# Heads of 64: the value's high and low part as one weight of 128 columns, two passes for three, and the halves added on VectorE

## The chip, the cores and the metric

The kernel runs on one core of one Trainium2 chip. The metric is the device time of one launch in microseconds. The profile is one execution of the kernel before, read instruction by instruction: PE is TensorE's matmul, PEld its weight load, DVE is VectorE, ACT is ScalarE, POOL is GpSimd, SP issues most transfers.

## What is computed

The reference is a whole small model over 512 rows of width 1024, in fp32. The first half has two layers: an attention, a cross attention on a memory of 256 rows, and a gated feed-forward network each. The second half is one layer with a "forgetting" attention beside a pooling mixer, and a convolved feed-forward network. The change touches the two attentions whose values are 64 wide and whose scores are dense and causal:

```
# first layer (MLA): 16 heads, queries and keys 96 wide, values 64 wide
logits = jnp.einsum('bqhd,bkhd->bhqk', q_blk, k).astype(jnp.float32) * scale
logits = jnp.where(causal[None, None], logits, -jnp.inf)
p = jax.nn.softmax(logits, axis=-1).astype(v.dtype)
return jnp.einsum('bhqk,bkhd->bqhd', p, v)
...
# second half (fox): 8 heads, queries, keys and values 64 wide
s = s + Fi[..., None] - Fk[:, :, None, :]
s = jnp.where(qpos[:, None] >= kpos[None, :], s, -jnp.inf)
p = jax.nn.softmax(s, axis=-1)
return jnp.einsum('bhqk,bkhd->bqhd', p, v32)
```

## The kernel before

Every fp32 operand of a matmul is held as a pair of fp32r tiles, a high part and a low part. `split` (L157 to L161) makes a pair: ScalarE casts the source to the high part (L160), and VectorE subtracts the high part from the source for the low part (L161). `mm3` (L151 to L155) multiplies two pairs in three passes, high by high (L153), high by low (L154), low by high (L155).

`attention` (L666 and on) serves both stretches. Per head it has four steps. `s1` computes the scores of four row blocks (tile `s`, 12 matmuls), takes mask and row minimum in one operation on VectorE (L685, tile `P`, or `p` for the block of 256), and the exponential on ScalarE (L687). `norm` takes the reciprocal of the row sums on VectorE (L693) and multiplies on GpSimd (L696). `s2` transposes the probabilities on TensorE (L704, ten transposes, tiles `t`) and splits them into three pairs `pt`. `s3` multiplies by the values: one PSUM tile `o`, whose partitions 0 to 63 are the head's 64 columns, collects four key blocks by `mm3`, with 512, 384, 256 and 128 rows of queries; the weight is the 64 columns of the value (tile `v`), and the moving operand is `pt`. So one head has 12 matmuls for `o`, and then `split` writes half a pair of `ot`, which is the input of the projection after the attention.

The loop over heads is a software pipeline. Iteration h issues `s3(h - lag)`, `s2(h - 2)`, `norm(h - 1)`, `s1(h)`, and then other work that fills TensorE: for MLA the projections of queries and keys for two heads more at every even h below 14 (36 matmuls, tile `qk`), and by the tables `FILL_V` and `FILL_A` parts of the values and of the cross attention's keys and values (tiles `v`, `k`); for fox the pooling mixer (tile `pl`). The lag is 3 for MLA and 4 for fox. PSUM has 8 buffers that all tiles share. A scheduler at build time orders the instructions of each engine from this program; at run time each engine works through its own list, and waits at each instruction for what it needs.

MLA's attention lies at about 85 to 230 us of the span, fox at about 1700 to 1778 us. During MLA the low parts of the weights (`wl`, L122) are made on GpSimd.

Of the kernel before, what the change touches and what calls it, by code (L numbers as in the profile page):

```python
# [9 lines left out]
F = mybir.dt.float32  # L10
R = mybir.dt.float32r
# [3 lines left out]
OP = mybir.AluOpType  # L15
# [4 lines left out]
NT = 4  # L20
# [44 lines left out]
class K:  # L65
# [416 lines left out]
    def mla(self):  # L482
        nc, a = self.nc, self.a
        xd = a["x"][0].rearrange("(t p) d -> p t d", p=128)
        xs = []
        for t in range(NT):
            x = self.pg(F, "x0")
# [98 lines left out]
        V = {}  # L586
        st = {}

        def vproj(h, js=range(NT)):
            if js[0] == 0:  # L590
                st["v"] = self.use()
            u = st["v"]
            for j in js:
                p = self.ps("v")
                g, c = j // 2, slice((j % 2) * 128, (j % 2) * 128 + 128)
                for k in range(2):
                    self.mm3(p, [ckv[g][0][:, k, c], ckv[g][1][:, k, c]], [u[0][:, k], u[1][:, k]], k == 0, k == 1)
                V[h, j] = self.pair("v")
                self.split(V[h, j][:, 0], V[h, j][:, 1], p)

        kr = self.pair("kr")
        self.rope(krf, kr)
# [10 lines left out]
        for i in range(2):  # L613
            nc.scalar.dma_start(KF[i][0][64:96].bitcast(F), kr[64:96].bitcast(F))
            nc.scalar.dma_start(KF[i][1][32:64].bitcast(F), kr[32:64].bitcast(F))
        OT = []
        vproj(0)

        def proj(p):
# [35 lines left out]
        def fill(h):  # L655
            if h in FILL_V:
                vproj(1, FILL_V[h])
            self.fill(FILL_A.get(h, 0))
        self.attention(16, rowsel, lambda h: [V[h // 8, j][:, :, (h % 8) * 64:(h % 8) * 64 + 64] for j in range(NT)],
                       OT, scale, ahead,  # L660
                       None, fill)
        self.ahead, self.dma_ahead = AHEAD, DMA_AHEAD
        self.lo_eng = nc.vector
        return OT

    def attention(self, nh, rows, vals, OT, scale, ahead, before3=None, fill=None, lag=3):  # L666

        nc = self.nc
        A = {}

        def s1(h):
            q, k = rows(h)
            p0, p1, p2 = self.ps("s"), self.ps("s"), self.ps("s")
            sv = [p0[:, 0:128], p1[:, 0:256], p0[:, 128:512], p2[:, 0:512]]
            pa = self.pg(F, "P")
            pb = self.cp.tile([128, 256], F, tag="p1", bufs=3, name=self.nm("p1"))
            pv = [pa[:, 896:1024], pb, pa[:, 512:896], pa[:, 0:512]]
            sm = self.small(16, "st")
            for b in (3, 2, 0, 1):
                nk = (b + 1) * 128  # L680
                c = slice(b * 128, b * 128 + 128)
                self.mm3(sv[b], [q[:, 0, c], q[:, 1, c]], [k[:, 0, 0:nk], k[:, 1, 0:nk]], True, True)
            for b in (3, 2, 0, 1):
                nk = (b + 1) * 128
                nc.vector.tensor_tensor_reduce(out=pv[b], in0=sv[b], in1=self.mask[:, 512 - nk:512], scale=-scale,  # L685
                                               scalar=3.0e38, op0=OP.add, op1=OP.min, accum_out=sm[:, b:b + 1])
                nc.scalar.activation(pv[b], pv[b], AF.Exp, bias=sm[:, b:b + 1], scale=-1.0,  # L687
                                     accum_out=sm[:, 4 + b:5 + b])
            A[h] = dict(pv=pv, sm=sm)

        def norm(h):
            sm, pv = A[h]["sm"], A[h]["pv"]
            nc.vector.reciprocal(sm[:, 8:12], sm[:, 4:8])  # L693
            for b in (3, 2, 0, 1):
                nk = (b + 1) * 128
                nc.gpsimd.tensor_tensor(pv[b], pv[b], sm[:, 8 + b:9 + b].to_broadcast([128, nk]), op=OP.mult)  # L696

        def s2(h):
            pv = A[h]["pv"]
            t0, t1, t2 = self.ps("t"), self.ps("t"), self.ps("t")  # L700
            tv = [t0[:, 0:512], t1[:, 0:384], t2[:, 0:256], t1[:, 384:512]]
            for j in (3, 1, 2, 0):
                for b in range(j, 4):
                    nc.tensor.transpose(tv[j][:, (b - j) * 128:(b - j + 1) * 128], pv[b][:, j * 128:(j + 1) * 128],  # L704
                                        self.ident)
            g1, g0 = self.pair("pt"), self.pair("pt")
            g2 = self.cp.tile([128, 512], R, tag="pt2", bufs=2, name=self.nm("pt2")).rearrange("p (h n) -> p h n", h=2)
            self.split(g1[:, 0], g1[:, 1], t1)
            self.split(g2[:, 0], g2[:, 1], t2[:, 0:256])
            self.split(g0[:, 0], g0[:, 1], t0)  # L710
            A[h]["pt"] = [g0[:, :, 0:512], g1[:, :, 0:384], g2, g1[:, :, 384:512]]

        def s3(h):
            v, pt = vals(h), A[h]["pt"]
            o = self.ps("o")
            for j in range(NT):
                self.mm3(o[0:64, 128 * j:512], [v[j][:, 0], v[j][:, 1]], [pt[j][:, 0], pt[j][:, 1]], j == 0, j == 3)
            if h % 2 == 0:
                OT.append(self.pair("ot"))
            r = slice(64 * (h % 2), 64 * (h % 2) + 64)  # L720
            self.split(OT[h // 2][r, 0], OT[h // 2][r, 1], o[0:64])
            del A[h]

        for h in range(nh + lag):
            if 0 <= h - lag < nh:
                if before3 is not None:
                    before3(h - lag)
                s3(h - lag)
            if 0 <= h - 2 < nh:
                s2(h - 2)  # L730
            if 0 <= h - 1 < nh:
                norm(h - 1)
            if h < nh:
                s1(h)
                ahead(h)
            if fill is not None:
                fill(h)
# [107 lines left out]
    def fill(self, n=1):  # L845

        if self.kvs is None:
            self.kvs = self.xa_kv_steps()
        for _ in range(n):
            next(self.kvs, None)  # L850
# [536 lines left out]
    def second(self, xT, xn, xs):  # L1387
        nc, a = self.nc, self.a
        v = nc.vector
# [32 lines left out]
        p = fz[0]  # L1422
# [23 lines left out]
        vp = [self.ps("v") for _ in range(NT)]  # L1446
        for kk in range(4):
            u = self.use()
            for j in range(NT):
                c = slice(j * 128, j * 128 + 128)  # L1450
                for k in range(2):
                    x = xT[2 * kk + k]
                    self.mm3(vp[j], [x[:, 0, c], x[:, 1, c]], [u[0][:, k], u[1][:, k]], kk + k == 0, kk == 3 and k == 1)
        V = []
        for j in range(NT):
            V.append(self.pair("v"))
            self.split(V[j][:, 0], V[j][:, 1], vp[j])
        QF, KF = [], []

        def rings():  # L1460
# [24 lines left out]
        def pool_mm(g, mp, pw):  # L1485
            p = self.ps("pl")
            self.mm3(p, [pw[0][:, g], pw[1][:, g]], [mp[:, 0], mp[:, 1]], True, True)
            o = mixed[4 + g] = self.pair("mx")
            sc = self.col2[:, 64 + g:65 + g]
            nc.scalar.activation(o[:, 0], p, AF.Copy, scale=sc)  # L1490
            v.scalar_tensor_tensor(o[:, 1], p, sc, o[:, 0].bitcast(F), op0=OP.mult, op1=OP.subtract)

        OT = []
# [11 lines left out]
        def pools(h):  # L1505
            if h == min(FILL_P):
                pw.append(self.use())
            for g in FILL_P.get(h, ()):
                pool_mm(g, mps[g], pw[0])
        self.attention(8, rows, lambda h: [V[j][:, :, h * 64:h * 64 + 64] for j in range(NT)], OT, 1.0, before,  # L1510
                       fill=pools, lag=4)
        self.ahead, self.dma_ahead = AHEAD, DMA_AHEAD
        for k in range(4):
# [158 lines left out]
```

## Time and profile before

| what | value |
|---|---|
| time, median of 3 runs | 2203.94 us (2202.64 to 2204.45) |
| the profiled execution | 2198.25 us, span 2196.2 us |
| mean granted clock of TensorE | 0.987 of full |
| PE busy | 2144.8 us, 98% of the span |
| VectorE, ScalarE, GpSimd busy | 1353.9, 898.8, 294.2 us |

The span runs from the first to the last instruction on the chip; the profiled execution has 2.05 us around it. Busy time of PE is the union of its matmuls, which overlap in the pipeline: the cost of one matmul among others is the time from its start to the start of the next, and not the duration in its row.

### The profile page before, as it was taken

To read this page: it belongs to the slowest core of one execution; us is meant where nothing else is said; L and a number is where in the kernel's file an instruction comes from. 1 tells how busy PE (TensorE), PEld (TensorE's weight loads), DVE (VectorE), ACT (ScalarE), POOL (GpSimd) and SP (SyncE) were. 2 spreads that over 40 slices of the span, in tenths; PEclk is the share of its full clock that TensorE was granted. 3 is DMA by queue.
4 is the path that set the end of the run, shared out by engine and by line. 5 is a ranking of instruction groups with operands and counts; after the bars stand their busy time and mean duration, and the time that the engine had idled before them with its cause. 6 is when DMAs were issued, how large, how long until landed. Compare 5 with 4: busy or idle time off the path is not lost.

```text
span 2196.2 us, 30394 instructions
## 1 busy us (share of the span) xinstructions
PE 2144.8 (98%) x11668; PEld 1798.5 (82%) x11668; DVE 1353.9 (62%) x2819; ACT 898.8 (41%) x1636; POOL 294.2 (13%) x290
## 2 busy tenths in 40 slices
PE   8899999999999999899999999999999999999998
PEld 7789898988888887776689898888888879888886
DVE  5776566835237267898875855436377676765634
ACT  3677444312224043456634332224324555443521
POOL 0355100000000012365500000000003210000002
PEclk9999999999999998999999999999999999999999
DMA  5223613355334132230251355534320144433311
GB/s 192 63 66 93 208 58 115 104 156 162 88 109 141 54 97 64 77 113 29 82 163 59 106 173 173 153 115 163 106 58 20 45 125 145 141 91 100 128 58 39
DMA packets 253393, 232.28 MB, mean 106 GB/s; under 512 B 14656, under 2 KB 219840, under 8 KB 253248
## 3 DMA queue, kind: packets, MB, share of 16 engines
q1 hardware_dynamic: 246240, 213.93, 31.9%
q10 hardware_dynamic: 7008, 16.41, 2.2%
q8 instruction: 92, 1.51, 0.3%
q14 instruction: 53, 0.43, 0.1%
HBM read 220.80 MB, written 6.82 MB: 104 GB/s over the span
## 4 chain that ended last, share of the span: by engine, by line
PE 85%; DVE 6%; issue 1%; ACT 1%; POOL 1%; DMA 0%; ACTq 0%; SPq 0%; DVEq 0%; POOLq 0%
PE fm L154 14%; PE fm L153 14%; PE fm L155 14%; PE acc L154 9%; PE acc L155 9%; PE acc L153 9%; PE v L153 1%; PE v L154 1%; PE o L153 1%; PE v L155 1%; PE o L154 1%; PE o L155 1%; PE s L1241 1%; PE tp L232 1%; PE s L155 1%
## 5 line engine op out<-in xcount | busy, mean ns | idle before, releaser
L154 PE MATMUL fm<-xT,wh 128*128 128x512 f32 (+3 forms) x1640 | 589.6, 361 | 0.4
L155 PE MATMUL fm<-xT,wl 128*128 128x512 f32 (+3 forms) x1640 | 588.9, 359 | 0.0
L153 PE MATMUL fm<-xT,wh 128*128 128x512 f32 (+3 forms) x1640 | 588.5, 361 | 0.1
L122 DVE TENSOR_TENSOR wl<-raw,wh 128x1024 fp32r<-128x1024 f32 (+1 forms) x299 | 357.0, 1218 | 93.4 <-ACT wh L121 63.9
L121 ACT CAST wh<-raw 128x1024 fp32r<-128x1024 f32 (+2 forms) x339 | 339.0, 1039 | 65.6 <-PE acc L154 18.9
L154 PEld LDWEIGHTS fm<-xT,wh 128*128 128x128 f32 (+2 forms) x1640 | 307.9, 188 | 48.5 <-DVE xT L250 1.6
L155 PEld LDWEIGHTS fm<-xT,wl 128*128 128x128 f32 (+2 forms) x1640 | 307.9, 188 | 46.9
L153 PEld LDWEIGHTS fm<-xT,wh 128*128 128x128 f32 (+2 forms) x1640 | 307.1, 188 | 47.9 <-DVE xT L249 0.6
L122 POOL TENSOR_TENSOR wl<-raw,wh 128x1024 fp32r<-128x1024 f32 (+1 forms) x40 | 93.7, 2348 | 1228.5 <-ACT wh L121 614.5
L153 PE MATMUL acc<-wh,hs 128*128 128x512 f32 x528 | 205.6, 389 | 0.0
L154 PE MATMUL acc<-wl,hs 128*128 128x512 f32 x528 | 205.4, 389 | 0.0
L155 PE MATMUL acc<-wh,hs 128*128 128x512 f32 x528 | 204.9, 389 | 0.0
L967 DVE TENSOR_TENSOR hT<-sil,fm 128x512 f32<-128x512 f32 x44 | 30.3, 688 | 228.9 <-PE fm L155 215.5
L966 ACT ACTIVATE sil<-fm 128x512 f32<-128x512 f32 x44 | 26.3, 598 | 300.6 <-PE fm L155 283.5
L950 DVE SCALAR_TENSOR_TENSOR cv<-fm,cw,cv 128x511 f32<-128x511 f32 x88 | 65.7, 748 | 81.7 <-ACT cv L948 80.5
L153 PEld LDWEIGHTS acc<-wh,hs 128*128 128x128 f32 x528 | 99.1, 188 | 20.7
L155 PEld LDWEIGHTS acc<-wh,hs 128*128 128x128 f32 x528 | 99.1, 188 | 20.5
L154 PEld LDWEIGHTS acc<-wl,hs 128*128 128x128 f32 x528 | 99.1, 188 | 20.4
L153 PE MATMUL acc<-wh,ot 128*128 128x512 f32 x288 | 112.5, 391 | 0.0
L155 PE MATMUL acc<-wh,ot 128*128 128x512 f32 x288 | 112.1, 389 | 0.0
L154 PE MATMUL acc<-wl,ot 128*128 128x512 f32 x288 | 112.1, 389 | 0.0
L217 ACT ACTIVATE x<-x,mv 128x1024 f32<-128x1024 f32 x20 | 24.9, 1243 | 147.4 <-DVE mv L216 147.4
(366 smaller groups left out, 3660.0 us busy)
## 6 DMA issues: line engine op xcount, KB each, us to landing
raw<-in_ffn_w_in_dram SPq DMA_DIRECT2D x88, 512.0 KB, 4.0
mw<-in_mod_w_dram SPq DMA_DIRECT2D x48, 512.0 KB, 4.8
raw<-in_ffn_w_down_dram SPq DMA_DIRECT2D x44, 512.0 KB, 3.3
raw<-in_ffn_up_dram SPq DMA_DIRECT2D x44, 512.0 KB, 4.0
raw<-in_xa_w_kv_dram SPq DMA_DIRECT2D x32, 512.0 KB, 3.9
raw<-in_ffn_down_dram SPq DMA_DIRECT2D x22, 512.0 KB, 3.3
raw<-in_xa_w_q_dram SPq DMA_DIRECT2D x16, 512.0 KB, 5.3
raw<-in_xa_w_o_dram SPq DMA_DIRECT2D x16, 512.0 KB, 3.2
```

The lines of the kernel that those rows point to most:

```text
L121: self.nc.scalar.copy(hi[:, :n], raw[:, :n])
L122: self.lo_eng.tensor_tensor(lo[:, :n], raw[:, :n], hi[:, :n].bitcast(F), op=OP.subtract)
L153: mm(out, l[0], r[0], start=first, stop=False, **kw)
L154: mm(out, l[0], r[1], start=False, stop=False, **kw)
L155: mm(out, l[1], r[0], start=False, stop=last, **kw)
L217: ops.append(lambda: nc.scalar.activation(x, x, AF.Identity, bias=mv[:, 3:4], scale=mv[:, 2:3]))
L232: nc.tensor.transpose(st["ps"][:, g, tl * 128:(tl + 1) * 128], xs[2 * grp + tl][:, (f + g) * 128:(f + g + 1) * 128], self.ident)
L950: nc.vector.scalar_tensor_tensor(y[:, sh:], p[:, :S - sh], w[:, 2 - sh, c:c + 1], y[:, sh:], op0=OP.mult, op1=OP.add)
L966: nc.scalar.activation(s, g, AF.Silu)
L967: nc.vector.tensor_tensor(hT[j // 2][:, j % 2], s, u, op=OP.mult)
L1241: mm(p[32 * gq:32 * gq + 32, 0:nk], D3[:, i, hf], mv[:, gq, 0:nk], start=False, stop=i == 2, skip_group_check=True)
```

## The change

The values are stored head by head, 64 columns of the high part and then the 64 of the low part of the same head, so that one weight of 128 columns holds both. The product of a key block is then two matmuls in place of three, one with the high and one with the low part of the probabilities as the moving operand. Partitions 0 to 63 of `o` collect what the high part of the value gives, partitions 64 to 127 what the low part gives (the product of both low parts, which `mm3` left out, is now in it). ScalarE copies partitions 64 to 127 to an SBUF tile `oy`, VectorE adds partitions 0 to 63 to it, and the pair of `ot` is split from `oy` in SBUF and not from `o` in PSUM.

```
+    @staticmethod
+    def hp64(v):
+        return v.rearrange("p (a b c) -> p a b c", a=8, b=2)
+
+    def vsplit(self, p):
+        v = self.pg(R, "v")
+        x = self.hp64(v)
+        self.split(x[:, :, 0], x[:, :, 1], p.rearrange("p (a c) -> p a c", a=8))
+        return v
...
# where the values are made, MLA
-                V[h, j] = self.pair("v")
-                self.split(V[h, j][:, 0], V[h, j][:, 1], p)
+                V[h, j] = self.vsplit(p)
...
# where the values are made, fox
-            V.append(self.pair("v"))
-            self.split(V[j][:, 0], V[j][:, 1], vp[j])
+            V.append(self.vsplit(vp[j]))
...
# s3
             for j in range(NT):
-                self.mm3(o[0:64, 128 * j:512], [v[j][:, 0], v[j][:, 1]], [pt[j][:, 0], pt[j][:, 1]], j == 0, j == 3)
+                for i in range(2):
+                    nc.tensor.matmul(o[:, 128 * j:512], v[j], pt[j][:, i], start=j == 0 and i == 0, stop=j == 3 and i == 1)
             if h % 2 == 0:
                 OT.append(self.pair("ot"))
             r = slice(64 * (h % 2), 64 * (h % 2) + 64)
-            self.split(OT[h // 2][r, 0], OT[h // 2][r, 1], o[0:64])
+            y = self.cp.tile([128, 512], F, tag="hp", bufs=3, name=self.nm("oy"))
+            nc.scalar.copy(y[r], o[64:128])
+            nc.vector.tensor_tensor(y[r], o[0:64], y[r], op=OP.add)
+            self.split(OT[h // 2][r, 0], OT[h // 2][r, 1], y[r])
```

In the changed kernel the matmuls of `o` are at L729, the copy at L734, the add at L735; L685, L693 and L704 of the kernel before are L696, L704 and L715 there. The order of SP's transfers is the same in both. On the other engines the lists differ in the two attention stretches alone.

VectorE, MLA, where the value product of head 4 (`o_1500` before, `o_1496` after) is split while the scores of head 7 (`P_1546`, `p_1547` before, `P_1541`, `p_1542` after) are reduced. In the kernel before:

```order
L161 TENSOR_TENSOR ot_1513<-o_1500,ot_1513 64x512
L161 TENSOR_TENSOR kf_587<-qk_1454,kf_587 64x512
L161 TENSOR_TENSOR qf_583<-qk_1471,qf_583 64x512
L161 TENSOR_TENSOR pt_1529<-t_1517,pt_1529 128x512
L161 TENSOR_TENSOR pt_1531<-t_1518,pt_1531 128x256
L161 TENSOR_TENSOR pt_1530<-t_1516,pt_1530 128x512
L685 ISA P_1546,st_1548<-s_1545,cst 128x512
```

In the changed kernel:

```order
L735 TENSOR_TENSOR oy_1506<-o_1496,oy_1506 64x512
L161 TENSOR_TENSOR pt_1526<-t_1513,pt_1526 128x256
L161 TENSOR_TENSOR qf_583<-qk_1467,qf_583 64x512
L696 ISA p_1542,st_1543<-s_1539,cst 128x256
L161 TENSOR_TENSOR ot_1505<-oy_1506,ot_1505 64x512
L161 TENSOR_TENSOR pt_1524<-t_1512,pt_1524 128x512
L161 TENSOR_TENSOR pt_1525<-t_1511,pt_1525 128x512
L696 ISA P_1541,st_1543<-s_1540,cst 128x512
```

The subtraction for `ot` has become an add for `oy` and a later subtraction; the reduction of the score block of 256, which came last of its head's four, now stands ahead of both large `pt` of the head whose value product is next.

TensorE at the next head's value product (head 5: `o_1569` before, `o_1564` after), right behind the score matmuls of head 7. In the kernel before:

```order
L155 MATMUL s_1544<-kf_589,qf_585 128x256
L153 MATMUL o_1569<-pt_1530,v_751 64x512
L704 MATMUL t_1585<-cst,P_1417 128x128
L704 MATMUL t_1585<-cst,p_1418 128x128
...
L154 MATMUL o_1569<-pt_1530,v_751 64x512
L155 MATMUL o_1569<-pt_1530,v_751 64x512
```

In the changed kernel:

```order
L155 MATMUL s_1539<-kf_589,qf_585 128x256
L729 MATMUL o_1564<-pt_1525,v_751 128x512
L715 MATMUL t_1579<-cst,P_1413 128x128
L715 MATMUL t_1579<-cst,p_1414 128x128
L729 MATMUL o_1564<-pt_1525,v_751 128x512
L729 MATMUL o_1564<-pt_1524,v_761 128x384 x2
```

Both take one matmul with the high part of `pt` and then transposes of head 6 (`t_1585`, `t_1579`) until the low part is there. Before, all ten transposes stand in that gap; now two do, and the other eight come behind the value product.

## Rows read from the trace of the kernel before

**Rows 1.** The page: busy time of the engines; the chain that ended last, by engine.
```profile
PE 2144.8 (98%) x11668; PEld 1798.5 (82%) x11668; DVE 1353.9 (62%) x2819; ACT 898.8 (41%) x1636; POOL 294.2 (13%) x290
...
PE 85%; DVE 6%; issue 1%; ACT 1%; POOL 1%; DMA 0%; ACTq 0%; SPq 0%; DVEq 0%; POOLq 0%
```

**Rows 2.** Windows: stretch, its length, busy time (instructions), granted clock, DMA share, GB/s.
```profile
103.00:121.00 18.00, 18.00 (x123) 16.03 (x122) 13.94 (x36) 13.10 (x33) 9.53 (x11) 1.00 0.09 20
121.00:167.00 46.00, 43.79 (x327) 39.68 (x326) 35.99 (x99) 36.72 (x91) 28.09 (x31) 1.00 0.29 79
167.00:200.00 33.00, 32.96 (x250) 30.29 (x248) 21.63 (x55) 22.97 (x54) 16.45 (x17) 1.00 0.33 95
200.00:230.00 30.00, 29.46 (x223) 27.25 (x224) 15.02 (x35) 19.43 (x40) 20.45 (x16) 1.00 0.43 147
230.00:290.00 60.00, 60.00 (x272) 49.78 (x271) 36.91 (x69) 20.28 (x23) 0.00 (x0) 1.00 0.46 149
...
1749.00:1778.00 29.00, 27.13 (x185) 22.43 (x183) 22.70 (x55) 22.19 (x53) 8.26 (x12) 1.00 0.48 155
```

**Rows 3.** Timeline of PE, head 0's value product: start us, duration us, instruction.
```profile
102.82 0.39 PE L153 MATMUL o<-pt,v 128*64 128x512 f32 x1
...
103.50 0.34 PE L153 MATMUL o<-pt,v 128*64 128x384 f32 x1
...
104.02 0.28 PE L153 MATMUL o<-pt,v 128*64 128x256 f32 x1
...
104.36 0.22 PE L153 MATMUL o<-pt,v 128*64 128x128 f32 x1
...
104.54 0.29 PE L704 MATMUL t<-cst,P 128*128 128x128 f32 x1
```

**Rows 4.** Timeline of PE, matmuls with weights of 128 columns.
```profile
97.81 0.23 PE L153 MATMUL s<-kf,qf 96*128 96x128 f32 x1
97.87 0.28 PE L154 MATMUL s<-kf,qf 96*128 96x128 f32 x1
...
98.10 0.34 PE L153 MATMUL s<-kf,qf 96*128 96x256 f32 x1
...
98.51 0.28 PE L153 MATMUL qk<-ckv,wh 128*128 128x256 f32 x1
98.63 0.28 PE L154 MATMUL qk<-ckv,wh 128*128 128x256 f32 x1
...
1773.28 0.40 PE L154 MATMUL pl<-mp,wh 128*128 128x512 f32 x1
1773.52 0.40 PE L155 MATMUL pl<-mp,wl 128*128 128x512 f32 x1
```

**Rows 5.** Groups of the whole span, forms apart: busy us, mean ns; idle before, releaser.
```profile
L161 DVE TENSOR_TENSOR hs<-hT,hs 128x512 fp32r<-128x512 f32 x66 | 44.4, 686 | 24.9 <-ACT hs L160 24.7
L160 ACT CAST hs<-hT 128x512 fp32r<-128x512 f32 x66 | 39.8, 620 | 60.3 <-PE acc L154 27.7 <-PE acc L155 14.8 <-DVE wl L122 10.5
L161 DVE TENSOR_TENSOR ot<-o,ot 64x512 fp32r<-64x512 f32 x24 | 16.4, 681 | 8.8 <-ACT ot L160 8.6
L160 ACT CAST ot<-o 64x512 fp32r<-64x512 f32 x24 | 13.8, 577 | 9.4 <-PE o L155 8.2 <-PE s L155 0.6 <-DVE qf L161 0.3
```

**Rows 6.** Timeline of PE, three of its waits: in brackets idle time before and releaser.
```profile
126.81 0.45 PE L154 MATMUL o<-pt,v 128*64 128x512 f32 x1 [0.71 <-DVE pt L161]
156.42 0.45 PE L153 MATMUL o<-pt,v 128*64 128x512 f32 x1 [1.09 <-ACT pt L160]
1772.01 0.33 PE L704 MATMUL t<-cst,p 128*128 128x128 f32 x1 [1.38 <-POOL p L696]
```

**Rows 7.** Timelines of POOL and DVE: the same multiplication twice, and VectorE beside the second.
```profile
145.79 2.18 POOL L696 TENSOR_TENSOR P<-P,st 128x512 f32<-128x512 f32 x3 [4.73 <-DVE st L693]
151.95 3.01 POOL L696 TENSOR_TENSOR P<-P,st 128x512 f32<-128x512 f32 x3 [0.89 <-DVE st L693]
153.24 0.67 DVE L161 TENSOR_TENSOR rq<-rp,rq 128x512 fp32r<-128x512 f32 x1
```

More of the change, by code (lines that the diff above doesn't have):

```diff
@@ L658, in fill @@
             self.fill(FILL_A.get(h, 0))
-        self.attention(16, rowsel, lambda h: [V[h // 8, j][:, :, (h % 8) * 64:(h % 8) * 64 + 64] for j in range(NT)],
+        self.attention(16, rowsel, lambda h: [V[h // 8, j][:, (h % 8) * 128:(h % 8) * 128 + 128] for j in range(NT)],
                        OT, scale, ahead,
@@ L1509, in pools @@
                 pool_mm(g, mps[g], pw[0])
-        self.attention(8, rows, lambda h: [V[j][:, :, h * 64:h * 64 + 64] for j in range(NT)], OT, 1.0, before,
+        self.attention(8, rows, lambda h: [V[j][:, h * 128:h * 128 + 128] for j in range(NT)], OT, 1.0, before,
                        fill=pools, lag=4)
```

## The prediction

> **What bounds the kernel now.** I read the page first: PE is busy for 98% of the span, and the chain that ended last lies for 85% on it [rows 1]. So time is won where TensorE's work shrinks and nothing else becomes late. The change touches 24 heads, 16 in MLA and 8 in fox, so the second view is the busy time in windows over these two stretches [rows 2]. The reader should see three kinds of stretch there. From 103 to 121, 167 to 200 and 200 to 230 us PE is full or nearly so (idle 0, 0.04 and 0.54 us), and VectorE and ScalarE have room: fills of other work cover what is late. From 121 to 167 us (heads 2 to 7 have their value product there) PE idles 46.00 - 43.79 = 2.21 us, and VectorE and ScalarE are at 78 and 80%. From 1749 to 1778 us (heads 1 to 7 of fox) PE idles 1.87 us and the two others are at 78 and 77%. Behind MLA PE is busy for 60.00 of 60 us at a DMA share of 0.46, so what MLA wins is not lost again to a transfer there. The granted clock is 1.00, the level of 2.4 GHz, in all of these stretches before and behind, so no term below comes from the clock. Third, the waits of PE in the two loaded stretches [rows 6]: they end with a `pt` of VectorE or ScalarE, or with GpSimd's multiplication. That is the loop around TensorE: transposes, split of `pt`, value product, and on the other side scores, minimum, exponential, normalisation. The change shortens TensorE's part of it and lengthens the other engines' part.
>
> **What is removed.** Four matmuls of 12 per head, and their weight loads. Head 0's 12 take 104.54 - 102.82 = 1.72 us; by the starts of the four blocks one matmul takes 0.227, 0.173, 0.113 and 0.06 us at 512, 384, 256 and 128 rows [rows 3]. If the columns of the weight are free, a third goes, 0.57 us. Weights of 128 columns take 0.24 us at 512 rows (1773.28 to 1773.52), 0.12 at 256 (98.51 to 98.63), and at 128 rows 0.06 to 0.12 (three matmuls from 97.81 to 98.10, with 97.87 between) [rows 4]; 0.18 at 384 lies between its neighbours. At the dear end eight matmuls cost 2 x (0.24 + 0.18 + 0.12 + 0.12) = 1.32 us, and the gain is 0.40 us. I take 0.50, the middle: 24 x 0.50 = 12.0 us of TensorE's time, between 9.6 and 13.7.
>
> One rule would have the change win more. The Trainium skill ("TensorEngine Tiling (Array Packing)", Key Properties) says that a change of tiling mode drains TensorE, and weights of 64 columns might be run in such a mode. By that each head before would pay a drain on the way in and out, and the change would save it. The trace does not agree: from 104.36 us three matmuls of 0.06 us lead straight to the first transpose, whose operand is 128 wide, at 104.54 [rows 3], with no room for a drain. So nothing is added for it.
>
> **What is added.** Per head a copy on ScalarE from PSUM of 64 partitions by 512. Its nearest row is the cast of `ot` from PSUM, 577 ns. And an add on VectorE with one operand in PSUM and one in SBUF, nearest the subtraction for `ot` with such operands, 681 ns [rows 5]. The split that stays now reads SBUF; with both operands there the rows for `hs` have 620 and 686 ns against 577 and 681, so this costs some 0.05 us and counts as nothing [rows 5]. Over 24 heads ScalarE gets about 14 us and VectorE 16 us more. The 12 splits that now write the values head by head move as many elements as before; if the strided writes cost half as much again, it would be 12 x 0.3 = 3.6 us on either engine while PE does other heads' work, which I take as hidden: before 121 us VectorE and ScalarE idle 4 and 5 us of 18 [rows 2].
>
> **What waits.** The four evacuation steps follow one another: copy, add, cast, subtraction; before there were two. Behind the copy and the cast on ScalarE stand casts of `pt` and exponentials, behind the add and the subtraction on VectorE the subtractions of `pt` and the score reductions. The build puts other work between the four, so they need not be waited out. But the order shown above has a cost: at head 7 of MLA (likewise at 9, 11 and 15) the reduction of the score block of 256, which needs the last score matmul of its head, stands ahead of `ot` and of both large `pt` of head 5. TensorE takes head 5's first matmul right behind these scores and then has two transposes, not ten, to do until the low part of `pt` arrives. Before, the `pt` were reached earlier. Work that covered a wait (eight transposes of 128 columns, 0.5 to 1.0 us by the 0.06 to 0.12 us above) has moved behind it.
>
> **The sum by stretch**, each with the heads in it:
> - 103 to 121 us, 2 heads, full of fills: -1.0 us.
> - 121 to 167 us, 6 heads: PE's work falls to 43.79 - 3.0 = 40.8, VectorE's rises to 36.0 + 6 x 0.68 = 40.1, ScalarE's to 36.7 + 6 x 0.58 = 40.2 us. Three engines are level in a loop where each waits for the others, so PE's idle time grows; between all of the 3.0 won and none, I take half, -1.5.
> - 167 to 200 us, heads 8 to 11: the first two stand beside long fills (-1.0), the last two in short iterations without (0): -1.0.
> - 200 to 230 us, heads 12 to 15, with VectorE at half load: -2.0, less 0.5 for the wait at head 12's product, which has few fills: -1.5.
> - fox, head 0, under the fills before 1749 us: -0.5.
> - fox, heads 1 to 7 (1749 to 1778 us): PE falls to 27.13 - 3.5 = 23.6, VectorE rises to 22.7 + 7 x 0.68 = 27.5, ScalarE to 22.2 + 7 x 0.58 = 26.2 of 29 us. VectorE at 95% can hardly be waited for by nobody; against that, PE's largest wait there is for GpSimd [rows 6], which is not lengthened. +0.5.
>
> Together -5.0 us: the profiled execution of 2198.25 us (2196.2 and 2.05 around it) would take 2193.2. It lies 5.7 us below the median of the runs, so against the median of 2203.94 I forecast 2199 us, 0.23% faster.
>
> **Rivals.**
> - *TensorE paces everywhere*, and the waits are hidden: all 12.0 us, 2192. For it: PE at 98%, and idle time of PE of only 4.7 us in all the windows of attention, so little stood in the way. Against it: the levels of 40 us above.
> - *GpSimd and VectorE stand in each other's way.* The normalisation takes 2.18 us alone, and 3.01 us where a subtraction of VectorE with both operands in SBUF (0.67 us) lies within it [rows 7], 0.83 more. The subtraction for `ot` now has both operands in SBUF in each head; before, one was in PSUM. It falls on a multiplication where GpSimd is at work: 28.09 of 46 us [rows 2]. For the 13 heads of the loaded stretches at a share of about 0.6, that is 8 heads at 0.68 us, the subtraction's length, which TensorE waits for where it waits for GpSimd already: 5.4 us lost of the 5.0 won, 2204.3, no change. Against it: MLA's waits in these rows name `pt`, not GpSimd.
>   The Trainium skill ("SBUF — State Buffer", Who interferes with whom) has that rule: a VectorE instruction with two inputs in SBUF and a GpSimd instruction that reads SBUF block each other. The trace agrees, with 3.01 against 2.18 us.
> - *The chain of VectorE and ScalarE paces the two loaded stretches* (slower). Each of their 13 heads then gets longer by what is added: 0.68 us if only VectorE's add counts, 1.26 if the copy ahead of it does too. The other 11 heads win 5.5 us. At the middle, 0.97, it is 12.6 - 5.5 = +7.1, 2211; at 0.68 +3.3, at 1.26 +10.9. It decides for slower beyond no change (4.4 us) from 9.9 / 13 = 0.76 us a head. For it: the order shown, and 95% on VectorE in fox. Against it: per head 46/6 = 7.7 us pass from 121 to 167, and VectorE has work for 6.7 of them after.
>
> **How the numbers follow.** 0.2%, or 4.4 us, is about what a measurement of this kernel can tell from no change. The forecast, with losses that leave 2 to 9 us of gain, gets 0.50, and half of it is beyond 4.4 us. TensorE pacing everywhere gets 0.22, GpSimd 0.13, the chain 0.15. So faster 0.25 + 0.22 = 0.47, same 0.25 + 0.13 = 0.38, slower 0.15. The range begins with the full gain at 13 us, 2191, and ends at 2206.5, where it leaves out most of the chain's case and little else. The forecast's own range is 2195 to 2202.
>
> **What would show it.** Eight matmuls of `o` in 1.15 to 1.32 us per head in the trace after, the copy near 0.58 and the add near 0.68 us. PE's idle time grows from 2.21 us to about 3.7 between head 2's and head 8's product, with `pt` as the releaser, most at heads 5 and 7; in fox it grows from 1.87 to about 5.9. MLA's end comes some 5 us earlier, and fox takes as long as before. If the normalisation's three parts last 2.9 us in most heads and PE waits for them, GpSimd was it; if an iteration without fill takes 0.8 us longer with VectorE busy throughout, the chain. The forecast is wrong if PE's idle time stays as it was, or if it grows by more than the 0.5 us that a head wins.

## The result, and the profile after

The changed kernel takes 2213.82 us (median of 5 runs, 2212.37 to 2216.50) against 2202.64 for the kernel before beside it: ratio 1.0055, interval 1.0043 to 1.0066, so it is slower by 11.2 us. The profiled executions lie further apart, 2216.50 against 2198.25, since the one after is the longest of its five runs and the one before lies below all five runs beside it. What follows compares these two where a stretch is named, and medians where a whole kernel is.

The page after, busy time and the chain that ended last, to be read against [rows 1]:

```profile
PE 2144.9 (97%) x11572; PEld 1801.9 (81%) x11572; DVE 1375.3 (62%) x2843; ACT 914.6 (41%) x1660; POOL 297.5 (13%) x290
...
PE 84%; DVE 6%; ACT 2%; POOL 1%; issue 1%; DMA 0%; ACTq 0%; SPq 0%; POOLq 0%; DVEq 0%
```

There are 96 matmuls fewer, and yet PE is as long busy as before (2144.9 against 2144.8 us): the rest of them ran longer. The windows show where (columns as in [rows 2]):

```profile
121.00:167.00 46.00, 37.97 (x227) 34.70 (x225) 35.16 (x82) 32.02 (x77) 24.06 (x25) 0.85 0.23 61
167.00:200.00 33.00, 30.72 (x241) 29.84 (x241) 25.39 (x66) 28.03 (x66) 17.97 (x16) 1.00 0.28 77
200.00:230.00 30.00, 27.94 (x197) 26.15 (x196) 20.79 (x52) 22.09 (x52) 16.56 (x19) 0.94 0.34 105
230.00:290.00 60.00, 60.00 (x299) 51.07 (x298) 34.54 (x46) 27.88 (x34) 10.26 (x5) 1.00 0.59 194
```

From 121 to 167 us PE now idles 8.03 us where it idled 2.21, and the granted clock is 0.85 where it was 1.00. A mark in the program turns this into a sum: the transposes of `mem` that stand right ahead of head 8's value product begin at 165.57 us before and at 178.53 after. The window from 92 us to that mark, before and then after:

```profile
92.00:165.57 73.57, 71.36 (x513) 64.66 (x513) 58.37 (x157) 58.87 (x147) 44.92 (x49) 1.00 0.23 60
```

```profile
92.00:178.53 86.53, 75.74 (x495) 69.86 (x494) 68.37 (x166) 63.71 (x154) 45.72 (x49) 0.92 0.19 49
```

Idle time of PE grows from 2.21 to 10.79 us: +8.6. A clock of 0.92 over 86.53 us costs 6.9 us. Eight heads' matmuls are shorter by 4.1 us. That is +11.4 of the 12.96 us by which the mark is later; the other 1.5 were there before head 0's product (104.33 against 102.82 us). The busy time agrees: it grew by 4.4 us where 2.6 less was due (4.1 were taken away, and at 92 us the work stands 1.5 us further back), so 7.0 us went into longer matmuls. As for the 1.5 us, from 84 to 92 us the granted clock is 0.79 against 0.96, and it is 0.79 in e9 below too, whose kernel differs from the one before only behind head 0's product; so these 1.5 us are not put down to the change. The mark is nearly all of MLA's loss: the projection behind MLA begins at 260.97 us against 248.78, 12.2 later. Fox adds some 4 us more: its head 0's product comes 13.3 us later than before, the projection behind it 17.0.

TensorE's own part came out as costed. Eight matmuls of `o` for head 2, and the first transpose behind them (timeline of PE):

```profile
122.37 1.37 PE L729 MATMUL o<-pt,v 128*128 128x512 f32 x8
123.58 0.29 PE L715 MATMUL t<-cst,P 128*128 128x128 f32 x1
```

That is 1.21 us against 1.72 [rows 3], 0.51 won per head. The added operations, and the subtraction that moved to SBUF (groups, forms apart):

```profile
L161 DVE TENSOR_TENSOR ot<-oy,ot 64x512 fp32r<-64x512 f32 x24 | 20.3, 845 | 5.9 <-ACT ot L160 5.4
L735 DVE TENSOR_TENSOR oy<-o,oy 64x512 f32<-64x512 f32 x24 | 16.3, 681 | 11.2 <-ACT oy L734 10.9
...
L734 ACT COPY oy<-o 64x512 f32<-64x512 f32 x24 | 14.0, 582 | 9.7 <-PE o L729 9.3
```

Copy and add are at the forecast 0.58 and 0.68 us. The subtraction has 845 ns in the mean against 681 [rows 5]; 8 of the 24 are above 0.75 us, together 3.9 us more than before. The waits of PE (timeline of PE, idle time and releaser in brackets) are to be read against [rows 6]:

```profile
130.33 0.50 PE L729 MATMUL o<-pt,v 128*128 128x512 f32 x1 [2.03 <-ACT pt L160]
132.09 0.47 PE L715 MATMUL t<-cst,p 128*128 128x128 f32 x1 [1.14 <-POOL p L707]
149.81 0.50 PE L729 MATMUL o<-pt,v 128*128 128x512 f32 x1 [2.36 <-ACT pt L160]
...
169.83 0.50 PE L729 MATMUL o<-pt,v 128*128 128x512 f32 x1 [2.28 <-ACT pt L160]
```

The rows with `o` are the products of heads 3, 5 and 7. Behind 149.81 a further wait of 1.44 us for VectorE's `pt` follows. At head 5, VectorE and beside it GpSimd (timelines):

```profile
148.50 0.42 DVE L696 CUSTOM_DVE_ANT_0 p<-s,cst 128x256 f32<-128x256 f32 x1
...
148.85 1.86 DVE L161 TENSOR_TENSOR ot<-oy,ot 64x512 fp32r<-64x512 f32 x1
150.64 1.27 DVE L161 TENSOR_TENSOR pt<-t,pt 128x512 fp32r<-128x512 f32 x2
...
147.81 2.36 POOL L122 TENSOR_TENSOR wl<-raw,wh 128x1024 fp32r<-128x1024 f32 x1
```

This is the place that the order showed: the reduction of 256, then the subtraction for `ot`, then both large `pt`. The subtraction takes 1.86 us in place of 0.69; GpSimd's `wl` ends at 150.17 us, and the subtraction some 0.5 us behind it, at 150.71. It explains the wait of 1.44 us, behind two transposes, for VectorE's `pt`.

The three long waits themselves end with a `pt` of ScalarE, and its list shows why. At head 3 (timelines of VectorE and ScalarE):

```profile
127.94 0.67 DVE L735 TENSOR_TENSOR oy<-o,oy 64x512 f32<-64x512 f32 x1
...
126.44 0.58 ACT L734 COPY oy<-o 64x512 f32<-64x512 f32 x1
127.05 0.38 ACT L160 CAST pt<-t 128x256 fp32r<-128x256 f32 x1
128.70 0.62 ACT L160 CAST ot<-oy 64x512 fp32r<-64x512 f32 x1 [1.28 <-DVE st L704]
129.23 1.05 ACT L160 CAST pt<-t 128x512 fp32r<-128x512 f32 x2
```

The cast of `ot` now needs VectorE's add, which ends at 128.61 us, and the casts of the large `pt` stand behind it in ScalarE's list. So ScalarE idles 1.28 us (the row names the reciprocal, which follows the add on VectorE), and TensorE waits for the `pt` behind. At heads 5 and 7 it idles 0.45 and 0.99 us in the same place; there 0.51 us of it or less is ScalarE's own issue of a transfer (147.49 and 167.59 us), and at head 7 the rest is the add. What follows the wait at head 3 is in the windows of 2 us:

```profile
128.00:130.00 2.00, 0.30 (x3) 0.10 (x1) 1.65 (x5) 1.30 (x3) 1.17 (x2) 1.00 1.10 253
130.00:132.00 2.00, 0.61 (x2) 0.27 (x2) 2.00 (x4) 0.28 (x1) 2.00 (x3) 0.76 0.60 116
132.00:134.00 2.00, 1.91 (x8) 1.82 (x9) 1.61 (x9) 0.98 (x2) 0.03 (x1) 0.50 0.00 0
134.00:136.00 2.00, 2.00 (x11) 2.00 (x10) 0.51 (x2) 1.98 (x9) 0.00 (x0) 0.50 0.28 65
136.00:138.00 2.00, 2.00 (x7) 1.71 (x7) 1.54 (x4) 1.26 (x3) 1.85 (x3) 0.54 0.66 197
138.00:140.00 2.00, 2.00 (x19) 2.00 (x18) 1.25 (x5) 0.54 (x1) 0.90 (x2) 1.00 0.03 8
```

PE is busy for 0.91 of the 4 us from 128 to 132, and when work comes back the clock stands at 0.50, which is 1.2 GHz, until about 138 us. Matmuls of the same form at either clock (timeline of PE):

```profile
136.33 0.63 PE L154 MATMUL s<-kf,qf 96*128 96x512 f32 x1
136.75 0.63 PE L155 MATMUL s<-kf,qf 96*128 96x512 f32 x1
...
172.50 0.40 PE L154 MATMUL s<-kf,qf 96*128 96x512 f32 x1
172.74 0.40 PE L155 MATMUL s<-kf,qf 96*128 96x512 f32 x1
```

From start to start it is 0.42 us at half clock and 0.24 at full. So this wait is paid twice, once as idle time and once in the matmuls behind it. Head 5's is followed by half clock in the same way, head 7's is not.

### The profile page after: what moved, and what is told of

It is laid out like the page before. It is cut to its first block, busy times and chain, and to the rows that moved or that the text cites. A ratio compares the mean times of both kernels' runs of the same rounds, so it can differ in the third digit from the quotient of the medians.

```text
span 2214.4 us, 30220 instructions
## 1 busy us (share of the span) xinstructions
PE 2144.9 (97%) x11572; PEld 1801.9 (81%) x11572; DVE 1375.3 (62%) x2843; ACT 914.6 (41%) x1660; POOL 297.5 (13%) x290
## 4 chain that ended last, share of the span: by engine, by line
PE 84%; DVE 6%; ACT 2%; POOL 1%; issue 1%; DMA 0%; ACTq 0%; SPq 0%; POOLq 0%; DVEq 0%
PE fm L154 14%; PE fm L153 14%; PE fm L155 14%; PE acc L154 9%; PE acc L155 9%; PE acc L153 9%; PE o L729 1%; PE v L153 1%; PE v L154 1%; PE v L155 1%; PE t L715 1%; PE s L1256 1%; PE s L153 1%; PE s L155 1%; PE s L154 1%
```

## The experiments

Theory A, formed on the trace above: the longer evacuation of the value product (two steps more between ScalarE and VectorE) makes TensorE wait, and the clock falls in the waits. Within it, theory P says that the blocking between VectorE and GpSimd is the larger part, theory O that the place in the order is. Theory B is the rival: the two passes themselves cost the time. Each kernel was timed beside the kernel before; "mark" is where the transposes of `mem` begin in its profile, with PE's idle time and the granted clock from 92 us to there. Each mark is of one execution, and these lie up to 6 us from their kernel's median (e2's 4.5 above, e10's 4.9 below), so marks that differ by a microsecond or two tell little.

| kernel | median us (before beside it) | ratio, 95% interval | mark us | idle us | clock |
|---|---|---|---|---|---|
| before | | | 165.57 | 2.21 | 1.00 |
| changed | 2213.82 (2202.64) | 1.0055, 1.0043 to 1.0066 | 178.53 | 10.79 | 0.92 |
| e1 evacuation alone | 2212.82 (2203.15) | 1.0049, 1.0037 to 1.0061 | 174.32 | 6.74 | 0.96 |
| e2 passes alone | 2195.35 (2203.15) | 0.9974, 0.9964 to 0.9983 | 164.99 | 3.94 | 1.00 |
| e3 sum in PSUM | 2206.77 (2203.15) | 1.0024, 1.0015 to 1.0033 | 171.91 | 7.42 | 0.96 |
| e4 late evacuation | 2214.59 (2203.15) | 1.0058, 1.0045 to 1.0072 | 176.91 | 8.39 | 0.90 |
| e5 low to low | 2213.06 (2200.81) | 1.0057, 1.0044 to 1.0070 | 178.71 | 8.58 | 0.90 |
| e6 late, low to low | 2207.74 (2200.81) | 1.0029, 1.0018 to 1.0041 | 173.72 | 7.28 | 0.94 |
| e7 late, sum in PSUM | 2207.30 (2200.81) | 1.0032, 1.0018 to 1.0045 | 173.16 | 6.29 | 0.94 |
| e8 gaps filled | 2217.79 (2200.81) | 1.0075, 1.0059 to 1.0091 | 177.50 | 8.16 | 0.98 |
| e9 VectorE's operation alone | 2206.24 (2203.24) | 1.0021, 1.0010 to 1.0031 | 169.33 | 3.74 | 1.00 |
| e10 passes and copy | 2208.26 (2203.24) | 1.0019, 1.0010 to 1.0029 | 171.92 | 6.13 | 0.91 |
| e11 add on GpSimd | 2208.52 (2203.24) | 1.0029, 1.0020 to 1.0037 | 172.49 | 7.24 | 0.94 |
| e12 halves added later | 2208.47 (2202.42) | 1.0032, 1.0020 to 1.0044 | 163.55 | 2.72 | 0.98 |
| e13 late work spread | 2210.55 (2201.17) | 1.0036, 1.0022 to 1.0049 | 163.66 | 2.73 | 0.98 |

**e1 and e2** take the change apart.

```
# e1, on the kernel before
-            self.split(OT[h // 2][r, 0], OT[h // 2][r, 1], o[0:64])
+            nc.scalar.copy(y[r], o[0:64])
+            nc.vector.tensor_tensor(y[r], o[0:64], y[r], op=OP.max)
+            self.split(OT[h // 2][r, 0], OT[h // 2][r, 1], y[r])
...
# e2, on the changed kernel
-            nc.scalar.copy(y[r], o[64:128])
-            nc.vector.tensor_tensor(y[r], o[0:64], y[r], op=OP.add)
-            self.split(OT[h // 2][r, 0], OT[h // 2][r, 1], y[r])
+            self.split(OT[h // 2][r, 0], OT[h // 2][r, 1], o[0:64])
```

> The evacuation alone: three passes and weights of 64 columns as before, but ScalarE copies the product from PSUM to an SBUF tile, VectorE takes the maximum of PSUM and copy (the same number, so the output is unchanged), and the pair is split from SBUF. Theory A (the longer evacuation of the value product makes TensorE wait for the probabilities' pairs, and the clock falls in the gaps): slower than before by 10 to 20 us, idle time of PE in MLA far above before's 3.4 us, stretches of granted clock 0.5 as in the changed kernel. Theory B (the two passes themselves, through weights of 128 columns or their PSUM tile, cost the time): within 3 us of before.

> The passes alone: two matmuls per block with weights of 128 columns as in the changed kernel, but the pair is split from partitions 0 to 63 in PSUM as before; the part of the low half of the values is left out of the output. Theory A: faster than before by 6 to 12 us (24 heads at 0.5 us less what waits grow), clock 1.00 through MLA. Theory B: slower than before by about as much as the changed kernel, 8 to 12 us.

The evacuation alone loses 9.7 us, a little less than the 10 to 20 expected; the passes alone win 7.8. Theory B is out. The two don't add up: -7.8 and +9.7 make +1.9, and the changed kernel has +11.2.

**e3 and e4** ask which property of the evacuation costs.

```
# e3, on the changed kernel
-            nc.vector.tensor_tensor(y[r], o[0:64], y[r], op=OP.add)
-            self.split(OT[h // 2][r, 0], OT[h // 2][r, 1], y[r])
+            nc.vector.tensor_tensor(o[0:64], o[0:64], y[r], op=OP.add)
+            self.split(OT[h // 2][r, 0], OT[h // 2][r, 1], o[0:64])
...
# e4, on the changed kernel: copy, add and split of s3 as a function evac
             if 0 <= h - 2 < nh:
                 s2(h - 2)
+            if 0 <= h - lag < nh:
+                evac(h - lag)
```

> The changed kernel with the sum written back to partitions 0 to 63 of the PSUM tile and the pair split from there, so that no operation of VectorE for the value product has both operands in SBUF; number of operations and their order nearly the same. Theory P (VectorE's subtraction and GpSimd block each other, seen as a subtraction of 1.86 us in place of 0.69): 4 to 8 us faster than the changed kernel. Theory O (the place of the add and the split ahead of the large pt in the order is what costs): within 2 us of the changed kernel.

> The changed kernel with copy, add and split of the value product issued behind the transposes and splits of the next head's probabilities, so that on ScalarE and VectorE they stand behind the large pt. Theory O: 6 to 14 us faster than the changed kernel, PE's waits for ScalarE's pt gone, clock 1.00 in most of MLA. Theory P: within 3 us of the changed kernel, subtractions of 1 to 2 us still there, and waits for GpSimd in place of those for pt.

The sum in PSUM gives 7 us back, the late evacuation nothing: the long waits for ScalarE's `pt` are gone, and others have come. In e3 the subtraction is short again (groups):

```profile
L735 DVE TENSOR_TENSOR o<-o,oy 64x512 f32<-64x512 f32 x24 | 16.5, 689 | 7.6 <-ACT oy L734 7.4
L161 DVE TENSOR_TENSOR ot<-o,ot 64x512 fp32r<-64x512 f32 x24 | 16.4, 683 | 5.2 <-ACT ot L160 4.6
```

So theory P's forecast came true, 7 us of the 11. Yet the 7 us can't all be put down to the blocking. The build reordered TensorE too: at head 5's product eight transposes stand in the gap where the changed kernel has two, and the wait of 1.44 us is gone. And the three long waits for ScalarE's `pt` are still there without any blocking, 2.00, 2.19 and 1.90 us; at head 3 ScalarE again idles 1.29 us ahead of the cast of `ot`, until the add is done.

In e4, from 157 us on, three shorter waits follow one another (timeline of PE; window):

```profile
159.13 0.36 PE L153 MATMUL s<-kf,qf 128*128 128x256 f32 x1 [1.43 <-DVE kf L161]
...
160.58 0.47 PE L729 MATMUL o<-pt,v 128*128 128x512 f32 x1 [0.86 <-DVE qf L161]
162.14 2.18 PE L729 MATMUL o<-pt,v 128*128 128x512 f32 x7 [1.09 <-DVE pt L161]
...
161.00:174.00 13.00, 11.21 (x45) 10.06 (x44) 7.72 (x24) 5.58 (x16) 5.95 (x8) 0.50 0.22 57
```

Half clock lies behind them for 13 us, the longest such stretch up to any mark in these runs. So a single long wait is not needed for it.

**e5, e6 and e7** look for an evacuation without these costs.

```
# e5, on the changed kernel in place of copy, add and split (e6: the same at the place of e4; e7: e3 and e4 together)
+            lo = OT[h // 2][r, 1]
+            self.split(OT[h // 2][r, 0], lo, o[0:64])
+            nc.vector.tensor_tensor(lo, o[64:128], lo.bitcast(F), op=OP.add)
```

> Two passes as in the changed kernel, but the halves are added otherwise: partitions 0 to 63 are split into the pair from PSUM as before, and VectorE adds partitions 64 to 127 from PSUM to the low part. One operation more on VectorE, none on ScalarE, no operation with both operands in SBUF, no step between ScalarE and VectorE more than before. If the loss lies in the four steps between ScalarE and VectorE and in the blocking beside GpSimd: 2 to 6 us faster than before, between the passes alone (7.8 us faster) and before, clock about 1.00 through MLA. If VectorE's added 0.68 us a head is what costs: within 2 us of the run with the sum in PSUM, 3 to 5 us slower than before.

> The run above with the split and the add of the value product issued behind the next head's pt. If their place in the order matters: 2 to 4 us faster than the run above. If not: within 2 us of it, or slower where the reciprocal comes later.

> The late evacuation with the sum written back to PSUM, so both corrections of the changed kernel at once. Theory O (place in the order counts once the blocking beside GpSimd is gone): 2 to 6 us faster than the sum in PSUM alone, so at or below the time of before. Theory P (blocking was the larger part, the place counts for nothing): within 2 us of the sum in PSUM alone.

e5 is a miss for me: one operation on VectorE, no blocking, no step more between the engines, and it is as slow as the changed kernel. Its VectorE at head 3, and TensorE's wait (timelines):

```profile
126.81 0.67 DVE L161 TENSOR_TENSOR ot<-o,ot 64x512 fp32r<-64x512 f32 x1
127.40 0.67 DVE L161 TENSOR_TENSOR pt<-t,pt 128x512 fp32r<-128x512 f32 x1
128.11 0.69 DVE L735 TENSOR_TENSOR ot<-o,ot 64x512 fp32r<-64x512 f32 x1
128.83 1.02 DVE L161 TENSOR_TENSOR pt<-t,pt 128x256 fp32r<-128x256 f32 x2
...
129.91 1.25 PE L729 MATMUL o<-pt,v 128*128 128x512 f32 x7 [2.36 <-DVE pt L161]
```

VectorE goes from one to the next without a pause, and the add stands between the `pt` that the product waits for. With the split and add behind the `pt` (e6) 5 us come back. For the sum in PSUM the place makes no difference (e7 against e3: 1.0032 and 1.0024, intervals that overlap). So the place counts where it puts an operation ahead of the `pt` that are due, and neither of the two places tried wins.

**e8** asks what the clock costs.

```
# e8, on the changed kernel, ahead of the loop over j in s3
+            if nh == 16 and h in (3, 5, 7, 11):
+                for _ in range(8):
+                    nc.tensor.matmul(o, v[2], pt[2].rearrange("p h n -> p (h n)"), start=True, stop=True)
```

> The changed kernel with eight useless matmuls of 512 rows (some 1.9 us at full clock) ahead of the value products of heads 3, 5, 7 and 11 of MLA, where TensorE waited 2.0 to 2.4 us; the real ones overwrite their PSUM tile, so the output is unchanged. The transposes move behind these value products, and the reduction of the block of 256 comes last of its four again except at head 9. Theory C (a wait of 2 to 4 us costs as much again by the half clock that follows it): clock near 1.00 in these stretches, MLA 4 to 10 us shorter, though TensorE does 7.4 us more work. Rival: the waits cost their own length only, so the time is within 2 us of the changed kernel or up to 7 us longer.

The clock up to the mark rises from 0.92 to 0.98, so 1.7 us are lost to it instead of 6.9, and the mark comes 1.0 us earlier although TensorE does useless work ahead of it. But the idle time falls by 2.6 us only (one wait for VectorE's `pt` is 3.10 us now), MLA ends 1.2 us earlier and not the 4 to 10 expected, and the whole kernel is some 4 us slower than the changed one against the kernel before (ratios 1.0075 and 1.0055). That lies in the range of the rival, by which the waits cost their own length only. So the times of e8 don't tell the two apart; that the clock costs time rests on the matmuls at half clock above.

**e9 to e11** put single operations to the test.

```
# e9, on the kernel before
             self.split(OT[h // 2][r, 0], OT[h // 2][r, 1], o[0:64])
+            nc.vector.tensor_tensor(y[r], o[0:64], OT[h // 2][r, 0].bitcast(F), op=OP.add)
...
# e10, on the changed kernel in place of copy, add and split (e11: and a line that adds y[r] to the low part on GpSimd)
+            self.split(OT[h // 2][r, 0], OT[h // 2][r, 1], o[0:64])
+            nc.scalar.copy(y[r], o[64:128])
```

> The kernel before, three passes, with one more operation on VectorE per head that nothing waits for: partitions 0 to 63 of the product in PSUM plus the high part in SBUF, written to a tile that no one reads. Theory V (VectorE is full where a head's large pt are due, so each operation ahead of them is paid by TensorE, and once more by the clock): slower than before by 6 to 14 us, PE waiting for VectorE's pt near heads 3 and 8. Rival D (only the dependence of the pair on copy and add costs): within 3 us of before.

> The passes alone with ScalarE's copy of partitions 64 to 127 added, which no one reads (the low half of the values is left out of the output). Theory V: ScalarE has room, so within 2 us of the passes alone, 5 to 9 us faster than before. Rival (both engines are full): 3 to 8 us slower than the passes alone.

> Two passes, the pair split from partitions 0 to 63 in PSUM as before, ScalarE copies partitions 64 to 127, and GpSimd adds the copy to the low part. VectorE has as much work as before. Theory V: 3 to 8 us faster than before, between the passes with the copy and before. Rival: GpSimd's add stands ahead of its multiplication of the probabilities and waits for the copy, so TensorE's transposes wait for GpSimd, and the time is within 3 us of before or up to 5 us slower.

Theory V, as I had put it, missed three times. On three passes the operation on VectorE costs 0.21%, far less than the 0.83% between e2 and e5 for an operation of the same size on two passes (there the projection needs its result, here nothing does). ScalarE's copy, for which I saw room, costs 0.45% on top of e2. The waits tell the difference. In e9 the two longest up to the mark are short of 1.4 us, and the clock stays at 1.00 (timeline of PE):

```profile
129.56 0.33 PE L704 MATMUL t<-cst,p 128*128 128x128 f32 x1 [1.33 <-POOL p L696]
...
159.89 0.45 PE L153 MATMUL o<-pt,v 128*64 128x512 f32 x1 [1.14 <-ACT pt L160]
```

In e10 ScalarE's copy stands ahead of the last `pt` of head 5, and TensorE waits 2.25 us for it; the clock up to the mark is 0.91:

```profile
140.03 0.58 ACT L735 COPY oy<-o 64x512 f32<-64x512 f32 x1
140.64 0.59 ACT L160 CAST pt<-t 128x512 fp32r<-128x512 f32 x1
...
141.28 0.50 PE L729 MATMUL o<-pt,v 128*128 128x512 f32 x1 [2.25 <-ACT pt L160]
```

**e12 and e13** take the evacuation out of the loop: for MLA alone ScalarE moves all 128 partitions in one copy in place of the cast, and split and add follow from head 12 on (e12) or head 11 on with part of it on GpSimd (e13).

```
# e12, MLA's s3 on the changed kernel, fox as before
+                nc.scalar.copy(Y[h // 2][:, 512 * (h % 2):512 * (h % 2) + 512], o)
...
+        def add_halves(i):
+            OT.append(self.pair("ot"))
+            for g in range(2):
+                r, y = slice(64 * g, 64 * g + 64), Y[i][:, 512 * g:512 * g + 512]
+                lo = OT[i][r, 1]
+                self.split(OT[i][r, 0], lo, y[0:64])
+                nc.vector.tensor_tensor(lo, lo.bitcast(F), y[64:128], op=OP.add)
```

> MLA alone with two passes, fox as before. In the loop ScalarE moves all 128 partitions of the product from PSUM to SBUF in one copy, in place of the cast, and VectorE does nothing for it; split and addition of the halves follow from head 12's iteration on, where the fills leave VectorE room. So TensorE's part of the loop is shorter by 0.5 us a head, and the other engines' part is not longer. If the lengthening of the loop on ScalarE and VectorE is the cause of the loss (theory V, in the form that any added operation there counts): 4 to 9 us faster than before, idle time of PE in MLA below 5 us and next to no half clock behind 92 us. Rival (the shorter matmul phase alone upsets the loop, or the late work delays the projection): between 2 us faster and 6 us slower than before, with waits for pt in the loop or for ot behind it.

> The halves added later, with that later work moved out of the way: it begins one iteration earlier (head 11's), and from the fifth pair on half of its subtractions and additions are on GpSimd, so four of VectorE's operations in place of ten stand ahead of the weights' low parts behind the loop. If the 4.0 us wait for those weights and the half clock after it were what took the gain: 2200 to 2204, 4 to 8 us faster than the run before it, MLA's end at or below before's 248.8 us. If the loop itself still costs (waits for ScalarE's pt with half clock behind them, though neither engine has more to do in it than before): 2205 to 2208, MLA's end above 251 us.

With nothing added on VectorE or ScalarE in the loop the marks come 2.0 and 1.9 us earlier than before, the only runs beside e2 in which they do, and the idle time is 2.7 us. That fits theory A, but it is half of the 4.1 us taken: each still has one wait of 1.90 us for ScalarE's `pt`, with half clock behind it. Both kernels lose later, and both expectations of a gain missed. In e12 the split and add stand on VectorE ahead of the low parts of weights that TensorE needs behind the loop, and two subtractions take 3.20 us in place of 1.4 (timelines of DVE and PE):

```profile
226.80 3.20 DVE L161 TENSOR_TENSOR ot<-y,ot 64x512 fp32r<-64x512 f32 x2 [0.77 <-ACT ot L160]
...
237.24 5.77 DVE L122 TENSOR_TENSOR wl<-raw,wh 128x1024 fp32r<-128x1024 f32 x5
...
238.51 0.77 PE L154 MATMUL v<-wl,mT 128*128 128x512 f32 x1 [3.96 <-DVE wl L122]
```

e13 breaks this wait into two (2.14 and 1.50 us for `wl`), has others of 1.70, 1.17 and 2.36 us from 185 to 198 us, and is no faster. No kernel tried that computes the whole output beats the kernel before.

## Why the prediction was wrong, by its steps

- **What is removed** was right: 0.51 us a head for the 0.50 taken; the passes alone (e2) win 7.8 of the 12.0 us.
- **What is added** was right in each duration but one: the split that reads SBUF "counts as nothing", and it was 845 against 681 ns in the mean, at most 1.86 us. The text had this mechanism, as a rival that costs up to 5.4 us; e3 wins 7 without it, though with another order of TensorE's. The Trainium skill ("SBUF — State Buffer", Who interferes with whom) says that a VectorE instruction with two inputs in SBUF and a GpSimd instruction that reads SBUF block each other. The trace agrees: 1.86 us beside `wl`, 683 ns where one operand is in PSUM. The rival looked for the loss in TensorE's waits for GpSimd; at head 5 it fell on the `pt` behind the blocked subtraction (1.44 us).
- **The sum by stretch** failed at 121 to 167 us, the step from which the rest follows. It forecast -1.5 us, with PE's idle time growing by half of the 3.0 us won. Up to the mark the idle time grew by 8.6 us, some 1.1 us a head where the text called the forecast wrong beyond 0.5. "Three engines are level" was read off busy time over the stretch; the waits come from single iterations (heads 3, 5, 7), where an added operation stands ahead of the `pt` that is due: on VectorE the subtraction, on ScalarE the copy and the cast of `ot`, ahead of which ScalarE at head 3 idles 1.28 us until VectorE's add is done. **What waits** had said that the steps need not be waited out, since the build puts other work between them. The order shown ahead of the prediction named the place at head 7's scores; I priced it at nothing beyond that half.
- **"No term below comes from the clock"** failed outright: 6.9 of the 13.0 us at the mark. The clock of 1.00 was read in a loop whose longest wait up to there was 1.09 us; the change made waits of 2.0 to 2.4 us, and two of the three are followed by some 7 us at 1.2 GHz. The same step hid why costs don't add: e2 and e9, which idle less than 4 us up to the mark, keep 1.00; e5 and e10, with one operation more than e2, idle 8.6 and 6.1 us and fall to 0.90 and 0.91. The length of a single wait doesn't tell: in e4, e6 and e7 none up to the mark is above 1.43 us, and the clock is 0.90 to 0.94.
- **The chain as a rival** had the right sign and the right engines. Its price of 0.68 to 1.26 us a head was too low: without the 1.5 us from before head 0, 11.5 us at the mark for the six heads from 2 to 7 are some 1.9 us each, clock included. It was given 0.15.

Four things stay open. How much each part of the evacuation costs: the build orders every engine anew with each edit (head 5's product has two transposes in its gap in the changed kernel, eight in e3, ten in e1, e2, e5 and e10), and no run holds the order fixed, so that the evacuation costs the time is shown, and how it divides into blocking, steps and place is in part argued. Why a wait of 2.25 us arises for ScalarE's copy alone (e10) is shown at head 5 only. The losses of the runs between the mark and the end were not taken apart one by one. And fox was not varied by itself; its part in the changed kernel, about 4 us, is read from one execution, with a wait of 1.89 us and half clock behind it.

## What to carry to other kernels

Where a loop passes between engines, don't weigh busy shares: take the iteration with the least fill, list what stands on VectorE and ScalarE ahead of the tile that TensorE waits for, and count an added operation there in full, with the time that its engine idles for its source. Then ask how much idle time gathers on TensorE, in one long wait or in several close together: here the half clock behind such waits cost 6.9 us beside 8.6 us of added idle time. Taking work from TensorE shortens what hid the other engines: an evacuation of copy, maximum and split cost 0.49% beside three passes (e1 against before), and one of copy, add and split 0.81% beside two (changed against e2).

## What the runs showed that was not expected

VectorE's subtraction with both operands in SBUF took up to 1.86 us for 0.69 beside one GpSimd instruction of 2.36 us, and ended 0.5 us behind it. One operation of 0.69 us more per head (e5 against e2), with the order that the build made of it, moved the mark by 13.7 us, with the granted clock going from 1.00 to 0.90. On GpSimd the addition of two SBUF tiles of 64x512 took 1319 ns (e11) where VectorE's takes about 690.
